# An encoder layer on one core: token operands of the FFN in overlapped rounds, and a four-tile last pass

## The chip, the core and the metric

The kernel runs on one core of a Trainium2 chip. Its engines are TensorE (PE, matrix products), VectorE (DVE), ScalarE (ACT), GpSimd (POOL) and SyncE (SP), which here issues every transfer. Each engine works through its own list of instructions in order and waits at semaphores for the others. The metric is the device time of one execution in microseconds.

## The reference, cut to what matters

One layer of a streaming encoder over 1024 tokens of width 1024, in float32, with a feed-forward width of 2816.

```python
x = x + 0.5 * _swiglu(_rmsnorm(x, n1_g[l]), ffn1_w_in[l], ffn1_w_out[l])
h = _rmsnorm(x, n2_g[l])
...   # one projection h @ w_in, then two attention branches o_a and o_b
merged = jax.nn.sigmoid(ga) * (o_a @ w_branch_a[l]) + jax.nn.sigmoid(gb) * (o_b @ w_branch_b[l])
x = x + merged @ w_out[l]
x = x + 0.5 * _swiglu(_rmsnorm(x, n3_g[l]), ffn2_w_in[l], ffn2_w_out[l])
return _rmsnorm(x, nf_g)
```

Here `_swiglu(x)` is `(silu(x @ gate) * (x @ up)) @ w_out`, and `_rmsnorm` divides each row by the root of its mean square and multiplies by a gain.

## The kernel before

Every product is made of three TensorE matmuls, since each operand is split into a high part (a cast on ScalarE, L82) and a remainder (a subtraction, L83, on VectorE, or on GpSimd where `w_eng` says so). The stages follow each other: FFN 1, a norm with its transposes (`norm_behind`), the projection with gates, attention A and B, the merge, FFN 2 and the final norm.

**First half of an FFN** (`ffn_in`). The product of tokens and input weights uses a form with seven block products in place of eight. Its token operands are b11, b21, b22 and four differences t1 to t4; they are made by `pair_operands` for four pairs of row tiles (p and p+4). For each pair: ScalarE squares both tiles (`rstds`, L166), VectorE normalises them (L244), GpSimd and VectorE make two differences each (L246 to L249, into two raw buffers), and TensorE transposes the seven operands in 28 steps of 128 columns (L254), each group of four into one bank named S, which ScalarE and VectorE then split. The weights have seven operands too, made by `ffn_weights` for each of NF = 22 column blocks i. Block i=0 is done in two halves of 256 columns, so that its first half needs pairs 0 and 1 alone: 14 products of 12 matmuls (L292). Later blocks take 512 columns. For i=0 GpSimd makes the remainders of the weights, later VectorE.

**Second half** (`out_rows`). A pass over two column tiles f adds to each of 8 row tiles, in two halves of 512 columns, a group of six matmuls (L118), and VectorE adds the bank into x (L226). The last pass of FFN 2 is taken row tile by row tile, each followed by its final norm (`scaled`) and the write of the output; GpSimd does two multiplications (L181, L182) for row tiles 1, 3 and 5, VectorE one instruction (L184) for the others. In the merge, column tiles go in pairs too, but the last two, i=6 and i=7, make a pass each (groups of three matmuls), the very last row tile by row tile, with `pair_operands` of FFN 2 after every pair.

**What sets the order.** The instruction order on each engine is laid out when the kernel is built, by a scheduler that runs the instructions through a timeline; code order and the pools' buffers bound it. All weights and some scratch come through one ring of five raw buffers of 128 x 1024 (`raw()`): a load into one waits until its last reader is done. The weight differences and the junk output of the Squares have a pool of their own, `sm`.

Of the kernel before, what the change touches and what calls it, by code (L numbers as in the profile page):

```python
# [43 lines left out]
class Layer:  # L44
# [114 lines left out]
    def rstds(self, tiles):  # L159
# [77 lines left out]
    def pair_operands(self, ops, x0, x1, gb, p):  # L237
# [12 lines left out]
        for n, src in (("b11", x0[:, :h]), ("b21", x0[:, h:]), ("b22", x1[:, h:]), ("t2", ta[:, h:]),  # L250
                       ("t1", ta[:, :h]), ("t3", tb[:, :h]), ("t4", tb[:, h:])):
            pt = self.bank("S")
# [6 lines left out]
    def ffn_weights(self, w_in, i):  # L259
# [5 lines left out]
        rg, ru = self.raw(), self.raw()  # L265
        for r, c in ((rg, i * P), (ru, F + i * P)):
            self.dma(r.rearrange("p (k c) -> p k c", k=KT), w_in[:, c:c + P].rearrange("(k p) c -> p k c", p=P))
        sm = [self.sm.tile([P, h], F32, tag=f"s{j}", name=self.uid(f"s{j}"), bufs=1) for j in range(4)]
        a11, a12, a21, a22 = rg[:, :h], rg[:, h:], ru[:, :h], ru[:, h:]
        for out, x, y, op in ((sm[0], a21, a22, ALU.add), (sm[1], sm[0], a11, ALU.subtract),  # L270
                              (sm[2], a11, a21, ALU.subtract), (sm[3], a12, sm[1], ALU.subtract)):
            nc.gpsimd.tensor_tensor(out, x, y, op)
        for j, src in enumerate((a11, a12, sm[1], sm[0], sm[2], sm[3], a22)):
            w = self.wp.tile([P, 2, h], F32R, tag=("whi", "wlo")[j % 2], name=self.uid("wop"), bufs=3)
            self.split(w[:, 0], w[:, 1], src, self.w_eng)
            yield w

    def ffn_in(self, w_in, ops, ph, g_d, first):
# [16 lines left out]
        for i in range(NF):  # L295
            self.w_eng = nc.gpsimd if i == 0 else nc.vector
            m = 256 if i == 0 else 512
            if i == 0:
                pairs = first()
                next(pairs)  # L300
                ws = list(self.ffn_weights(w_in, i))
                next(pairs, None)
            else:
                ws = self.ffn_weights(w_in, i)
            gh, gl = (ph.tile([P, SEQ], F32R, tag="t4", name=self.uid("g"), bufs=4) for _ in range(2))
# [34 lines left out]
    def ffn(self, x_d, w_in, w_out, g_d, ex, es_ex, first):  # L340
# [4 lines left out]
        kept = self.ffn_in(w_in, ops, ph, g_d, (lambda: iter((None,))) if first is None else lambda: first(ops, ph))  # L345
# [22 lines left out]
        for n, f in enumerate(range(0, NF - 2, 2)):  # L368
            cur = load((xo, go)[n % 2], f), weights(f)
            if f < NF - 4:  # L370
                self.out_rows(x, *cur, 0.5, range(NT))

# [461 lines left out]
    def merge(self, x, x1_d, gates_d, bra_d, ob, w_b, w_out, last, pool, pre):  # L834
# [3 lines left out]
        for i in range(KT):  # L838
            wh, wl = self.weights_cols(w_b, i * P, (i + 1) * P)
            gp, nb = (last, 1) if i == KT - 1 else (pool, 3)  # L840
# [26 lines left out]
            if len(cur) == 2 or i >= KT - 2:  # L867
                prev = (cur, [self.weights((w_out[f * P:(f + 1) * P, :], D)) for f in range(i + 1 - len(cur), i + 1)])
# [3 lines left out]
    def run(self):  # L872
# [14 lines left out]
        self.sm, es_sm = self.open("sm", bufs=1)  # L887
        ex, es_ex = self.open("ex", bufs=1, side="right")

        def first(ops, ph):  # L890
            xs = {}

            def load(ts):
                for t in ts:
                    xs[t] = ph.tile([P, D], F32, tag="t4", name=self.uid("x0"), bufs=4)
# [161 lines left out]
```

## Time and profile before

| | us |
|---|---|
| median of 3 runs | 2418.46 (2418.17 to 2420.24) |
| the profiled execution | 2418.89 |
| its span | 2417.1 |
| TensorE busy in the span | 2268.7 |
| VectorE busy | 1570.6 |
| ScalarE busy | 1015.6 |
| GpSimd busy | 572.2 |

Outside the span lie 1.8 us of the profiled execution. A timeline row gives the start, the duration, the engine, the line in the code, the operation with output and inputs, a count where equal neighbours are joined, and in brackets the idle time before it and who ended it. A row of windows gives the stretch, its length, busy time and number of instructions of PE, PEld (weight loads), DVE, ACT and POOL, then the granted TensorE clock as a share of full speed, the busy share of the DMA engines and GB/s; with a line as a filter, it has TensorE's share for that line alone. A row of a line gives count, shortest, median and longest duration in ns, and the first and last start. A row of instructions by line and shape gives the busy time and mean ns, and a row of transfers their number, KB of one, and median us from issue to landing.

### The profile page before, as it was taken

To read this page: it belongs to the slowest core of one execution; us is meant where nothing else is said; L and a number is where in the kernel's file an instruction comes from. 1 tells how busy PE (TensorE), PEld (TensorE's weight loads), DVE (VectorE), ACT (ScalarE), POOL (GpSimd) and SP (SyncE) were. 2 spreads that over 40 slices of the span, in tenths; PEclk is the share of its full clock that TensorE was granted. 3 is DMA by queue.
4 is the path that set the end of the run, shared out by engine and by line. 5 is a ranking of instruction groups with operands and counts; after the bars stand their busy time and mean duration, and the time that the engine had idled before them with its cause. 6 is when DMAs were issued, how large, how long until landed. Compare 5 with 4: busy or idle time off the path is not lost. (4 is left out here: it accounts for less than half of the span.)

```text
span 2417.1 us, 30580 instructions
## 1 busy us (share of the span) xinstructions
PE 2268.7 (94%) x10928; PEld 1894.5 (78%) x10928; DVE 1570.6 (65%) x2962; ACT 1015.6 (42%) x1973; POOL 572.2 (24%) x482
## 2 busy tenths in 40 slices
PE   3999999999999999998989999998699999999997
PEld 3877777778887987787778887876688888878886
DVE  5655555555656469798894388577665666656656
ACT  5444444420014554667734487532444444430002
POOL 3433333200014000222320143121433333310001
PEclk9999999999999999999999999998899999999999
DMA  3333333353422124455423241651333333354332
GB/s 104 116 105 105 105 105 105 105 212 145 157 93 104 36 75 120 106 131 133 119 67 98 100 157 40 217 171 48 105 104 114 105 105 105 117 197 166 127 117 105
DMA packets 204216, 280.81 MB, mean 116 GB/s; under 512 B 12064, under 2 KB 150304, under 8 KB 203552
## 3 DMA queue, kind: packets, MB, share of 16 engines
q1 hardware_dynamic: 204064, 278.86, 35.0%
q8 instruction: 86, 1.41, 0.2%
q14 instruction: 66, 0.54, 0.1%
HBM read 186.55 MB, written 79.69 MB: 110 GB/s over the span
## 5 line engine op out<-in xcount | busy, mean ns | idle before, releaser
L226 DVE SCALAR_TENSOR_TENSOR x<-S,x 128x512 f32<-128x512 f32 x432 | 292.1, 689 | 203.2 <-PE S L118 202.3
L82 ACT CAST whi<-raw 128x1024 fp32r<-128x1024 f32 (+1 forms) x92 | 87.6, 976 | 444.4 <-PE S L118 370.1
L118 PE MATMUL S<-wlo,goh 128*128 128x512 f32 x640 | 249.3, 389 | 0.0
L118 PE MATMUL S<-whi,gol 128*128 128x512 f32 x640 | 249.2, 389 | 0.0
L118 PE MATMUL S<-whi,goh 128*128 128x512 f32 x640 | 245.5, 394 | 3.4 <-DVE bigB L83 1.5
L292 PE MATMUL mm<-bigA,wop 128*128 128x512 f32 (+1 forms) x736 | 236.5, 384 | 10.8 <-ACT e L316 10.8
L83 DVE TENSOR_TENSOR wop<-s,wop 128x512 fp32r<-128x512 f32 x168 | 168.3, 1002 | 119.1 <-ACT wop L82 115.8
L292 PE MATMUL S<-bigA,wop 128*128 128x512 f32 (+1 forms) x736 | 233.0, 380 | 0.0
L83 DVE TENSOR_TENSOR wop<-raw,wop 128x512 fp32r<-128x512 f32 x126 | 114.1, 917 | 169.1 <-ACT wop L82 169.1
L83 POOL TENSOR_TENSOR wlo<-raw,whi 128x1024 fp32r<-128x1024 f32 (+1 forms) x32 | 68.2, 2130 | 524.8 <-ACT whi L82 516.1
L292 PEld LDWEIGHTS mm<-bigA,wop 128*128 128x128 f32 x736 | 136.6, 188 | 46.4 <-ACT e L316 20.3
L82 ACT CAST wop<-s 128x512 fp32r<-128x512 f32 x176 | 109.2, 622 | 142.4 <-PE mm L292 45.6
L118 PE MATMUL mm<-bigA,whi 128*128 128x512 f32 x384 | 155.3, 404 | 12.5 <-ACT whi L82 6.7
L292 PEld LDWEIGHTS S<-bigA,wop 128*128 128x128 f32 x736 | 136.5, 188 | 26.2
L118 PE MATMUL mm<-bigA,wlo 128*128 128x512 f32 x384 | 154.5, 403 | 2.3 <-POOL wlo L83 2.3
L323 POOL TENSOR_TENSOR e<-e,e 128x512 f32<-128x512 f32 (+1 forms) x46 | 57.2, 1243 | 419.1 <-ACT e L322 419.1
L118 PE MATMUL mm<-bigB,whi 128*128 128x512 f32 x384 | 154.7, 403 | 0.1
L118 PEld LDWEIGHTS S<-whi,goh 128*128 128x128 f32 x640 | 120.1, 188 | 35.9 <-DVE x L226 8.5
L586 POOL TENSOR_SCALAR p<-p,z 128x640 f32<-128x640 f32 (+7 forms) x128 | 92.7, 729 | 208.1 <-DVE z L585 141.4
L118 PEld LDWEIGHTS S<-whi,gol 128*128 128x128 f32 x640 | 120.2, 188 | 25.2
L292 PE MATMUL mm<-bigB,wop 128*128 128x512 f32 (+1 forms) x368 | 139.9, 380 | 0.0
L292 PE MATMUL S<-bigB,wop 128*128 128x512 f32 (+1 forms) x368 | 139.7, 380 | 0.0
(248 smaller groups left out, 5370.0 us busy)
## 6 DMA issues: line engine op xcount, KB each, us to landing
raw<-in_ffn_w_in_dram SPq DMA_DIRECT2D x88, 512.0 KB, 4.2
g_d<-g SPq DMA_DIRECT2D x80, 512.0 KB, 4.8
raw<-in_ffn_w_out_dram SPq DMA_DIRECT2D x44, 512.0 KB, 6.9
goh<-g_d SPq DMA_DIRECT2D x40, 512.0 KB, 5.1
gol<-g_d SPq DMA_DIRECT2D x40, 512.0 KB, 6.1
raw<-in_w_in_dram SPq DMA_DIRECT2D x28, 512.0 KB, 5.9
x<-in_x_dram SPq DMA_DIRECT2D x16, 512.0 KB, 6.6
x_d<-x SPq DMA_DIRECT2D x16, 512.0 KB, 2.6
```

Source lines behind the costliest of these rows:

```text
L82: self.nc.scalar.copy(hi, src)
L83: (eng or self.nc.vector).tensor_tensor(lo, src, hi.bitcast(F32), ALU.subtract)
L118: nc.tensor.matmul(out, lhsT=a, rhs=b, start=(i == 0), stop=(i == len(steps) - 1))
L226: nc.vector.scalar_tensor_tensor(xs, po, scale, xs, ALU.mult, ALU.add)
L292: nc.tensor.matmul(out, lhsT=l, rhs=r, start=start and j == 0, stop=j == len(steps) - 1, skip_group_check=True)
L323: nc.gpsimd.tensor_tensor(e3, e3, e5, ALU.add)
L586: nc.gpsimd.tensor_scalar(p, p, z, 1.0, ALU.mult, ALU.mult)
```

## The change

Five things are changed.

1. **Token operands.** `pair_operands` becomes a generator in two parts: norm and scaling, then differences and transposes. A new `all_operands` runs the first part of pair p+1 ahead of the second part of pair p. All four differences are GpSimd's, t1 and t4 in place, so a pair needs one raw buffer; the transposes go to the banks named mm and tp in turn instead of S.
2. **Weights.** `ffn_weights` takes raw buffers that are already being loaded, and makes its differences in place and in one tile `s` (two buffers for i>0, a raw buffer for i=0). For i=0 it is called after pair 2's second step in FFN 1, and ahead of `ffn` in FFN 2, whose first load is issued ahead of the merge's last rows.
3. **Junk.** The Squares write into a raw buffer, and the pool `sm` is gone. FFN 1 has six x tiles in flight instead of four.
4. **Merge.** The last two column tiles make one pass with groups of six matmuls.
5. **FFN 2's end.** The last pass takes four tiles f (16 to 19). g and weights of f = 18 and 19 wait in a spare 4 MB tile. Every final scaling is VectorE's.

```diff
@@ rstds
-            junk = self.sm.tile([P, D], BF16, tag="s0", name=self.uid("junk"), bufs=1)
+            junk = self.raw()
@@ pair_operands
-        ta, tb = self.raw(), self.raw()
-        nc.gpsimd.tensor_tensor(ta[:, :h], x1[:, :h], x0[:, :h], ALU.subtract)
-        nc.vector.tensor_tensor(ta[:, h:], x1[:, h:], ta[:, :h], ALU.subtract)
-        nc.gpsimd.tensor_tensor(tb[:, :h], x1[:, h:], x1[:, :h], ALU.subtract)
-        nc.vector.tensor_tensor(tb[:, h:], x0[:, h:], ta[:, h:], ALU.subtract)
...
-            pt = self.bank("S")
+        yield
+        b11, b21, b12, b22 = x0[:, :h], x0[:, h:], x1[:, :h], x1[:, h:]
+        tt = self.raw()
+        t3, t2 = tt[:, :h], tt[:, h:]
...
+        def sub(out, x, y):
+            nc.gpsimd.tensor_tensor(out, x, y, ALU.subtract)
+            return out
...
+            pt = self.bank(("mm", "tp")[turns % 2])
...
+        sub(t3, b22, b12)
+        turn("b11", b11)
+        turn("b21", b21)
+        turn("b22", b22)
+        t1 = sub(b12, b12, b11)
+        turn("t3", t3)
+        sub(t2, b22, t1)
+        turn("t1", t1)
+        turn("t2", t2)
+        turn("t4", sub(b21, b21, t2))
+
+    def all_operands(self, ops, tiles, gb, rows=None):
+
+        todo = []
+        for p in range(4):
+            if rows is not None:
+                rows(p)
+            g = self.pair_operands(ops, *tiles(p), gb, p)
+            next(g)
+            todo.append(g)
+            if p > 0:
+                next(todo[p - 1], None)
+            yield
+        next(todo[3], None)
@@ ffn
-        for n, f in enumerate(range(0, NF - 2, 2)):
+        end = 4 if big else 2
+        for n, f in enumerate(range(0, NF - 4, 2)):
             cur = load((xo, go)[n % 2], f), weights(f)
-            if f < NF - 4:
+            if f < NF - 2 - end:
                 self.out_rows(x, *cur, 0.5, range(NT))
+        f = NF - 4
+        if big:
+            spare = self.hp.tile([P, 8, SEQ], F32R, tag="bigA", name=self.uid("spare"))
...
+            cur = cur[0] + g, cur[1] + w
@@ the merge
-            if len(cur) == 2 or i >= KT - 2:
+            if len(cur) == 2:
@@ first (FFN 1)
+            raws = self.ffn_raw(io["ffn1_w_in"], 0)
+            load(pairs[4:6])
+            made = self.all_operands(ops, lambda p: (xs[p], xs[p + 4]), gb)
+            for p in range(4):
+                if p == 3:
+                    load(pairs[6:])
+                next(made)
+                if p == 2:
+                    self.w_eng = nc.gpsimd
+                    ws = list(self.ffn_weights(raws, self.raw()))
+            next(made, None)
@@ the final norm
-            self.scaled(x[:, t, :], x[:, t, :], gf, fin, t in (1, 3, 5))
+            self.scaled(x[:, t, :], x[:, t, :], gf, fin, False)
```

What this does to the order of instructions is seen at three places. Rows name line, operation, output and inputs; before, L246 and L248 are the token subtractions and L272 those of the weights, after, L252 and L309; L83 is a remainder.

GpSimd at the start, after the constants. Before:

```order
L83 TENSOR_TENSOR wop_130<-raw_118,wop_130 128x512
L83 TENSOR_TENSOR wop_133<-raw_118,wop_133 128x512
L272 TENSOR_TENSOR s_13_122<-raw_119 128x512
L272 TENSOR_TENSOR s_15_124<-raw_118,raw_119 128x512
L272 TENSOR_TENSOR s_14_123<-s_13_122,raw_118 128x512
L83 TENSOR_TENSOR wop_139<-s_13_122,wop_139 128x512
L272 TENSOR_TENSOR s_16_125<-raw_118,s_14_123 128x512
L83 TENSOR_TENSOR wop_136<-s_14_123,wop_136 128x512
L83 TENSOR_TENSOR wop_142<-s_15_124,wop_142 128x512
L83 TENSOR_TENSOR wop_145<-s_16_125,wop_145 128x512
L246 TENSOR_TENSOR raw_169<-x_7_110,x_6_108 128x512
L248 TENSOR_TENSOR raw_170<-x_7_110 128x512
```

After:

```order
L252 TENSOR_TENSOR raw_155<-x_7_107 128x512
L252 TENSOR_TENSOR x_7_107<-x_7_107,x_6_105 128x512
L83 TENSOR_TENSOR wop_283<-raw_115,wop_283 128x512
L83 TENSOR_TENSOR wop_286<-raw_115,wop_286 128x512
L252 TENSOR_TENSOR raw_155<-x_7_107 128x512
L252 TENSOR_TENSOR raw_225<-x_10_113 128x512
L252 TENSOR_TENSOR x_6_105<-x_6_105,raw_155 128x512
L252 TENSOR_TENSOR x_10_113<-x_10_113,x_9_111 128x512
L309 TENSOR_TENSOR raw_279<-raw_116 128x512
L252 TENSOR_TENSOR raw_225<-x_10_113 128x512
L309 TENSOR_TENSOR raw_279<-raw_279,raw_115 128x512
L309 TENSOR_TENSOR raw_116<-raw_115,raw_116 128x512
```

The token subtractions stood behind all weight work of block 0 and came two a pair; they now come first, four a pair, mixed with the weight work, and pair 0 and pair 1 stand close together.

TensorE at the end of the merge (L118 are the matmuls of the rows, S a bank, whi and wlo weights, gh and gl the gated activations; L254 and L260 transposes). Before, from the last matmuls of pair 0's rows on:

```order
L118 MATMUL S_15328<-whi_15295,gh_15160 128x512
L118 MATMUL S_15328<-wlo_15296,gh_15160 128x512
L118 MATMUL S_15328<-whi_15295,gl_15161 128x512
L254 MATMUL S_15356<-ident,x_14296 128x128 x4
L254 MATMUL S_15363<-ident,x_14296 128x128 x4
L254 MATMUL S_15370<-ident,x_14296 128x128 x4
L254 MATMUL S_15377<-ident,raw_15350 128x128 x4
L254 MATMUL S_15384<-ident,raw_15350 128x128 x4
L254 MATMUL S_15391<-ident,raw_15351 128x128 x4
L254 MATMUL S_15398<-ident,raw_15351 128x128 x4
L118 MATMUL S_15405<-whi_15295,gh_15160 128x512
```

After, where the first transposes stand:

```order
L118 MATMUL S_15321<-whi_15138,gh_15077 128x512
L118 MATMUL S_15321<-wlo_15139,gh_15077 128x512
L118 MATMUL S_15321<-whi_15138,gl_15078 128x512
L260 MATMUL tp_15261<-ident,x_14219 128x128 x4
L260 MATMUL mm_15268<-ident,x_14219 128x128 x4
L260 MATMUL tp_15275<-ident,x_14219 128x128 x4
L118 MATMUL S_15330<-whi_15132,gh_14889 128x512
L118 MATMUL S_15330<-wlo_15133,gh_14889 128x512
L118 MATMUL S_15330<-whi_15132,gl_14890 128x512
L118 MATMUL S_15330<-whi_15138,gh_15077 128x512
L118 MATMUL S_15330<-wlo_15139,gh_15077 128x512
L118 MATMUL S_15330<-whi_15138,gl_15078 128x512
```

Before, all seven transpose groups of a pair stood together between its rows and those of the next pair. Now the first three groups of pair 0 stand in the middle of pair 2's rows, and rows of six matmuls go on between them and the rest.

SP at the end of FFN 1 (x_d are the writes of x1, raw from in_w_in the first gate weights, goh and gol the g tiles of the last pass). Before:

```order
L79 DMA goh_5005<-g_d_91 128x1024
L79 DMA gol_5006<-g_d_91 128x1024
L79 DMA raw_5560<-in_w_in_dram 128x8x128
L79 DMA goh_5149<-g_d_91 128x1024
L79 DMA gol_5150<-g_d_91 128x1024
L79 DMA goh_5153<-g_d_91 128x1024
L79 DMA gol_5154<-g_d_91 128x1024
L79 DMA x_d<-x_3664 128x1024 x8
L79 DMA raw_5626<-in_w_in_dram 128x584
```

After:

```order
L79 DMA goh_4932<-g_d_91 128x1024
L79 DMA gol_4933<-g_d_91 128x1024
L79 DMA goh_5076<-g_d_91 128x1024
L79 DMA gol_5077<-g_d_91 128x1024
L79 DMA goh_5080<-g_d_91 128x1024
L79 DMA gol_5081<-g_d_91 128x1024
L79 DMA x_d<-x_3591 128x1024 x8
L79 DMA raw_5486<-in_w_in_dram 128x8x128
L79 DMA raw_5552<-in_w_in_dram 128x584
```

The load of the first gate weights stood ahead of the last four g loads and the eight writes; it now stands behind them.

## Rows read from the trace of the kernel before

**Rows 1.** Page, table of engines
```profile
PE 2268.7 (94%) x10928; PEld 1894.5 (78%) x10928; DVE 1570.6 (65%) x2962; ACT 1015.6 (42%) x1973; POOL 572.2 (24%) x482
```

**Rows 2.** Windows, all engines: the start, the merge, the tail
```profile
0.00:60.00 60.00, 22.48 (x136) 19.32 (x136) 33.07 (x65) 30.75 (x55) 20.87 (x22) 1.00 0.34 102
1672.50:1690.00 17.50, 10.09 (x39) 8.72 (x40) 12.75 (x22) 7.46 (x14) 2.50 (x2) 0.61 0.15 61
2390.00:2400.00 10.00, 8.47 (x36) 6.06 (x34) 9.61 (x29) 3.92 (x9) 3.85 (x3) 1.00 0.26 105
```

**Rows 3.** Timeline of TensorE over the first 62 us
```profile
28.48 2.79 PE L254 MATMUL S<-ident,x 128*128 128x128 f32 x12 [28.48 <-DVE x L244]
...
47.80 1.68 PE L292 MATMUL mm<-t,wop 128*128 128x256 f32 x12
...
60.55 0.42 PE L292 MATMUL mm<-b,wop 128*128 128x256 f32 x1 [0.68 <-ACT b L82]
```

**Rows 4.** First 40 us: transfer of x (transfers); timeline of ScalarE, then VectorE
```profile
x<-in_x_dram SPq DMA_DIRECT2D x6, 512.0 KB, 4.2
...
20.31 1.06 ACT L166 ACTIVATE junk<-x 128x1024 bf16<-128x1024 f32 x1
...
27.05 2.48 DVE L244 SCALAR_TENSOR_TENSOR x<-x,rs,raw 128x1024 f32<-128x1024 f32 x2
```

**Rows 5.** Timeline of TensorE at the merge; its matmuls there by line and shape
```profile
1678.32 2.82 PE L254 MATMUL S<-ident,x 128*128 128x128 f32 x12 [5.85 <-DVE x L244]
1682.73 3.74 PE L254 MATMUL S<-ident,raw 128*128 128x128 f32 x16 [1.59 <-DVE raw L247]
...
1695.20 2.35 PE L254 MATMUL S<-ident,x 128*128 128x128 f32 x12 [4.78 <-DVE x L244]
...
L118 PE MATMUL S<-wlo,gh 128*128 128x512 f32 x12 | 5.2, 436 | 0.0
```

**Rows 6.** Timeline of the tail: TensorE, GpSimd, VectorE
```profile
2403.93 0.39 PE L118 MATMUL S<-whi,gol 128*128 128x512 f32 x1
...
2402.09 2.40 POOL L181 TENSOR_TENSOR x<-x,gain 128x1024 f32<-128x1024 f32 x1
...
2402.36 2.15 DVE L173 TENSOR_TENSOR rs<-rs,rt 128x1 f32<-128x1 f32 x1
...
2407.01 0.68 DVE L226 SCALAR_TENSOR_TENSOR x<-S,x 128x512 f32<-128x512 f32 x1
...
2412.13 1.28 DVE L184 SCALAR_TENSOR_TENSOR x<-x,rs,gain 128x1024 f32<-128x1024 f32 x1
```

**Rows 7.** Windows of line 292 on TensorE alone
```profile
0.00:60.00 60.00, 7.78 (x48) 1.00 0.34 102
1733.00:1741.00 8.00, 7.30 (x49) 0.79 0.36 106
```

**Rows 8.** Timeline near 29.6 us: GpSimd, VectorE
```profile
29.61 1.27 POOL L246 TENSOR_TENSOR raw<-x,x 128x512 f32<-128x512 f32 x1 [4.44 <-DVE rs L169]
...
29.64 1.25 DVE L170 TENSOR_TENSOR rt<-rs 128x2 f32<-128x2 f32 x1
```

**Rows 9.** Lines 244, 247, 170; line 83 of VectorE from 28 to 62 us
```profile
L244 DVE SCALAR_TENSOR_TENSOR x<-x,rs,raw x16: 1276/1280/1285, 27.1 to 1727.0; 128x1024 f32<-128x1024 f32 x16
...
L247 DVE TENSOR_TENSOR raw<-x,raw x8: 676/1620/1736, 32.9 to 1729.8; 128x512 f32<-128x512 f32 x8
...
L170 DVE TENSOR_TENSOR rt<-rs x24: 142/160/2252, 25.9 to 2411.4; 128x1 f32<-128x1 f32 x16, 128x2 f32<-128x2 f32 x8
...
L83 DVE TENSOR_TENSOR bigB<-S,bigA x12: 674/682/692, 37.1 to 60.8; 128x512 fp32r<-128x512 f32 x12
```

**Rows 10.** Transition to the projection: SP, TensorE; the page's transfers
```profile
721.61 26.01 SPq L79 DMA_DIRECT2D x_d<-x  x8
...
747.80 0.47 PE L118 MATMUL mm<-bigA,whi 128*128 128x512 f32 x1
...
raw<-in_w_in_dram SPq DMA_DIRECT2D x28, 512.0 KB, 5.9
```

More of the change, by code (lines that the diff above doesn't have):

```diff
@@ L268, in ffn_weights, with sub @@
[L268 removed]
+        rg, ru = raws
         a11, a12, a21, a22 = rg[:, :h], rg[:, h:], ru[:, :h], ru[:, h:]
[L270 to L271 removed]
+        s1, s2 = s[:, :h], s[:, h:]
+        def sub(out, x, y, op=ALU.subtract):
             nc.gpsimd.tensor_tensor(out, x, y, op)
[L273 removed]
+        sub(s1, a21, a22, ALU.add)
@@ L295, in ffn_in @@
         for i in range(NF):
-            self.w_eng = nc.gpsimd if i == 0 else nc.vector
             m = 256 if i == 0 else 512
[L298 to L305, printed above, removed]
+            if i > 0:
+                self.w_eng = nc.vector
+                ws = self.ffn_weights(self.ffn_raw(w_in, i),
+                                      ph.tile([P, 1024], F32, tag="s", name=self.uid("s"), bufs=2))
+            elif ws is None:
+                ws = first(ops, ph)
+            gh, gl = (ph.tile([P, SEQ], F32R, tag="t4", name=self.uid("g"), bufs=self.t4) for _ in range(2))
             for c in range(0, 512, m):
@@ L367, in ffn @@
         go, es_go = self.open("go", bufs=1)
-        for n, f in enumerate(range(0, NF - 2, 2)):
+        end = 4 if big else 2
+        for n, f in enumerate(range(0, NF - 4, 2)):
             cur = load((xo, go)[n % 2], f), weights(f)
-            if f < NF - 4:
+            if f < NF - 2 - end:
                 self.out_rows(x, *cur, 0.5, range(NT))
+        f = NF - 4
+        if big:
+            spare = self.hp.tile([P, 8, SEQ], F32R, tag="bigA", name=self.uid("spare"))
+            g, w = [(spare[:, 2 * j], spare[:, 2 * j + 1]) for j in range(2)], []
+            for j in range(2):
+                for h in range(2):
+                    self.dma(g[j][h], g_d[f + j, h])
+                raw = self.raw()
+                self.dma(raw, w_out[(f + j) * P:(f + j + 1) * P, :])
+                w.append((spare[:, 4 + 2 * j], spare[:, 5 + 2 * j]))
+                self.split(*w[j], raw)
+            cur = cur[0] + g, cur[1] + w
+        else:
+            cur = load(go, f), weights(f)
         def close():
@@ L866, in merge @@
                 prev = None
-            if len(cur) == 2 or i >= KT - 2:
-                prev = (cur, [self.weights((w_out[f * P:(f + 1) * P, :], D)) for f in range(i + 1 - len(cur), i + 1)])
+            if len(cur) == 2:
+                prev = (cur, [self.weights((w_out[f * P:(f + 1) * P, :], D)) for f in (i - 1, i)])
                 cur = []
@@ L992, in run, with pair_rows @@
         self.dma(gb, io["n3_g"].partition_broadcast(P))
-        for t in pairs:
-            rows((t,))
-            self.dma(x2_d[t], x[:, t, :])
-            if t >= 4:
-                self.pair_operands(ops2, x[:, t - 4, :], x[:, t, :], gb, t - 4)
+        raws = self.ffn_raw(io["ffn2_w_in"], 0)
+        def pair_rows(p):
+            for t in (p, p + 4):
+                rows((t,))
+                self.dma(x2_d[t], x[:, t, :])
+        made = self.all_operands(ops2, lambda p: (x[:, p, :], x[:, p + 4, :]), gb, pair_rows)
+        for _ in range(4):
+            next(made)
+        self.w_eng = nc.gpsimd
+        ws = list(self.ffn_weights(raws, self.raw()))
+        next(made, None)
         es_m1.close()
-        x, rows, close = self.ffn(x2_d, io["ffn2_w_in"], io["ffn2_w_out"], g_d[1], ops2, es_ex, None)
+        x, rows, close = self.ffn(x2_d, io["ffn2_w_in"], io["ffn2_w_out"], g_d[1], ops2, es_ex, None, ws, True)
         fin, es_fin = self.open("fin", bufs=1)
@@ L1007, in run @@
         close()
-        es_sm.close()
 @with_exitstack
```

41 lines of the change are left out of this document (22 added, 19 removed).

## The prediction

> **What bounds the kernel now.** I read the page's table of engines first: TensorE is busy 94% of the span, VectorE 65%, GpSimd 24% [rows 1]. So the kernel is bound by TensorE, and an edit pays only where TensorE waits. The windows show where that is. In the first 60 us TensorE works 22.48 us, so 37.5 us are idle; between 1672.5 and 1690 it works 10.09 of 17.5, at a granted clock of 0.61; between 2390 and 2400 it works 8.47 of 10 [rows 2]. These are the three places the diff touches. Elsewhere the order of TensorE's instructions in the two feed-forward stages is the same in both kernels, so those hundreds of microseconds cancel.
>
> The timeline says who is waited for. At the start the first transposes begin at 28.48, released by VectorE's normalisation of the pair (L244), and TensorE runs without a gap from 60.55 [rows 3]. The cause lies earlier: the x tiles land in 4.2 us, but ScalarE squares the first one only at 20.31, behind casts of first-stage weights, and the normalisation comes at 27.05 [rows 4]. At the second FFN every pair of row tiles shows the same pattern: TensorE waits for the normalisation (5.85 us, then 4.78) and for a subtraction (1.59) [rows 5]; there are four such pairs, the eight waits add up to 27.3 us, and the pairs follow each other every 16 us or so, one after the other. At the end TensorE's last matmul starts at 2403.93 and ends by 2404.4, but the last evacuation runs at 2407.01, the last scaling at 2412.13, and the span closes 3.7 us after it, at 2417.1 [rows 6].
>
> **Start of FFN 1.** End of column block i=0 before: by 60 us TensorE had done 48 of the 168 matmuls of block 0 in 7.78 us [rows 7], and 88 of the 112 transposes (136 instructions in 22.48 us in all [rows 2], so 14.7 us for these). Left are 120 matmuls at 0.12 us (twelve take about 1.5 us [rows 3]) = 14.4, and 24 transposes at 0.17 = 4.0; from 60.55 that is 79.
>
> After: the Squares move ahead of the weights, so pair 0 is normalised at about 12.3: x issued at 0.7, landed about 5, then the 7 us from Square (20.31) to the end of its first scaling (27.05 plus 1.25), a little less since a cast and another Square stood in between [rows 4], and 1.2 for the second tile. What then sets the pace is GpSimd: it now does all 16 token subtractions, 4 weight subtractions and 7 remainders of the first block. Up to the subtraction that the first b11 product stands behind on TensorE (t2 of pair 3) those are 25 instructions at 1.25 us (its subtraction L246 takes 1.27 [rows 8]) = 31.3. VectorE's six scalings of pairs 1 to 3, 1.2 us each = 7.2, come in between (below). 12.3 + 31.3 + 7.2 = 50.8, with transposes about 52. Behind it stand 13 products of 12 matmuls (18.7 us; one is done earlier) and three groups of transposes, about 1.4: 72. Gain 7 (79 to 72). Bounds: 14, if the scalings cost GpSimd nothing; 0, if each of the 25 waits 0.3 us for small VectorE work as well.
>
> The 7.2 rests on this: in the trace two-input VectorE instructions do not run beside a GpSimd one. The tiny L170, normally 0.16 us, took 1.25 at 29.64 while GpSimd's L246 ran from 29.61; the evacuations, one input of which lies in PSUM, stayed at 674 to 692 ns [rows 9]. The scaling L244 itself never ran beside a busy GpSimd: 1276 to 1285 ns in all 16 cases [rows 8, 9]. So its behaviour there is inferred from L170 and L247 (676 to 1736 ns [rows 9]), the nearest rows. The Trainium skill (SBUF — State Buffer, section "SBUF: two separate sides") states that the two engines share one port pair as an exclusive lock, held for a whole instruction, and that a VectorE operation with two SBUF inputs takes part; by that rule L244 blocks and is blocked, which is the 52, and without it the chain ends near 45. The rows on L170 agree with it; no row shows L244.
>
> The four weight subtractions and remainders also feed i=1, whose raw buffers are freed late. By replay of the order its loads land about 51 and its products start after 72: hidden by 15 us and more.
>
> **Norm to projection.** The ring of five raw buffers now also takes the junk of the Squares, and the load of the first gate weights has moved behind the eight writes of x1 on the SP queue. Those writes are issued from 721.61 on for 26.01 us; before, 24 gate matmuls filled TensorE from 747.80 to 754.1, between transposes (their first [rows 10]). Now the load leaves at about 747.7, lands 5.9 later [rows 10], then cast and remainder, about 1 and 2.4: 757. TensorE has these 24 matmuls ahead of the last transposes and waits on them. At most their whole cover (24 x 0.23 = 5.5) and a bit is lost, +6; at least nothing, if the transposes of the last tiles were late anyway. I take +3.5, nearer to the whole because they stand in front in TensorE's order.
>
> **Merge and start of FFN 2.** The last two column tiles become one pass with six matmuls per group: eight row tiles of 2 x 6 x 0.227 = 2.72 us, starting about 1658.8 (of the two old passes' 96 matmuls 36, three lines of 12 [rows 5], come after TensorE's first wait, which begins at 1678.32 - 5.85 = 1672.47; the 60 before it take 13.6). 16 evacuations on VectorE vanish, hidden beside TensorE before too: nothing. Pair 0's rows are complete at 1664, its scaling at about 1671, while TensorE still has rows of later pairs to do: the first wait of 5.85 goes. Each further pair costs two row tiles (5.4) and seven groups of transposes (16 take 3.7 us [rows 5], so 6.5): the scalings end at about 1671, 1682.5 and 1695. After that of pair 2 GpSimd still has 16 instructions, 8 of tokens and 8 of weights: 20 us, and two scalings of pair 3 between, 2.4: 1717.4. Behind it stand again 20.1 us of products and transposes: block 0 ends at 1737.5. Before: by 1741 some 50 of 168 products were done (49 counted from 1733 to 1741 [rows 7]), so 118 x 0.12 = 14.2 more: 1755. Gain 17.8. Bounds: 28, if pair 2 is scaled 7 us earlier and the lock costs nothing; 8, if the pairs keep coming 16 us apart as now. The clock follows: it was granted at 0.61 of full speed in the first of these stretches [rows 2], where TensorE paused; that is part of both ends. The loads for i=1 wait for raw buffers freed at about 1717 and land 1722.5; their first use is about 1735: 12 us of cover.
>
> **Tail.** The last pass now spans four tiles of f, 5.44 us of TensorE per row tile against some 3.6 of VectorE (two evacuations, one scaling, six small ones). TensorE's three waits there, 1.5 us (10 less 8.47 [rows 2]), go. All scalings are VectorE's, so GpSimd's 2.40 us multiplication no longer holds up the small product at 2402.36 (2.15 us) [rows 6]. After the last matmul remain: evacuation 0.7, Square 1.25, mean, root and five small steps 1.7, scaling 1.28, write 3.7 = 8.6, against 12.7 now. Gain 4.1 + 1.5 = 5.7, between 4 and 7. The extra 4 MB for f = 18 and 19 is read hundreds of microseconds ahead, and its casts fall on ScalarE, 42% busy [rows 1]: nothing. Small reorderings inside the attention stage: nothing, up to 3 either way.
>
> **Sum.** -7 + 3.5 - 17.8 - 5.7 = -27. From the profiled execution's 2418.9 that is 2391.9; the median of the runs lies 0.4 lower, so 2391.5.
>
> **Rivals.**
> 1. *The lock eats it.* GpSimd waits about 0.4 us at each instruction (the nearest row is VectorE's L247, 0.68 alone and up to 1.74 beside L248 [rows 9]), and the pairs in effect still come one after another. FFN 1 gains nothing, FFN 2 only 17.8 - 6.4 = 11.4 or less: 0 + 3.5 - 11 - 5.7 = -13, 2405. For it: GpSimd's chain is long and VectorE's small steps have two inputs. Against: the evacuations, most of VectorE's work there, were not held up. It also covers the case that the change doesn't do what it says, the rounds not overlapping: FFN 2 then keeps its 16 us pitch and gains 8.
> 2. *No lock for the scaling.* -14 + 3.5 - 25 - 5.7 = -41: 2377.5. The 1285 ns maximum speaks for it, but only because the case never arose.
> 3. *Slower.* One mechanism: all subtractions and remainders now stand in a single file on GpSimd, with transposes and products behind, where before products of the first half filled gaps. If an instruction there costs 2.5 us instead of 1.25 (each alternating with a VectorE one), FFN 1's first product comes at 12.3 + 62.5 + 1 = 76, block 0 ends at 96: +16.5; FFN 2's at 1695 + 40 = 1735, block 0 at 1755: 0. With +3.5 and -5.7: +14, 2433. It decides from about 1.9 us per instruction on, since 41 instructions x 0.65 eat the 27. The longest two-input row here is about 1.75, so it is unlikely.
>
> **Chances.** Forecast (2380 to 2400) 0.55; rival 1 (2400 to 2411) 0.23; rival 2 (below 2380) 0.10; slower 0.07; within 0.2% of the old time, between rivals 1 and 3, 0.05. Differences below 0.2%, about 5 us, can't be told from none here. Faster 0.88, same 0.05, slower 0.07. The range reaches to rival 2's and rival 1's values: 2377 to 2408.
>
> **What would show it.** First transposes near 11 to 13 instead of 28.48, GpSimd near solid from 12 to 55, first run of b11 products near 52: the start. A TensorE gap of 3 to 6 us near 750: the gates. Near 1672 no 5.85 us wait, no gap-free TensorE later than 1718: the merge. Last scaling within 5 us of the last matmul: the tail. L244 above 1.3 us or GpSimd waiting for it: the lock. Wrong if GpSimd's pitch there is not near 1.25, or if the loads behind the raw ring are waited for.

## The result, and the profile after

The changed kernel takes 2391.03 us (median of 4 runs, 2389.85 to 2392.12) against 2419.35 for the kernel before on the same chip: a ratio of 0.9884, with a 95% interval from 0.9869 to 0.9898. 2391.5 was forecast, faster, with a range of 2377 to 2408. The profiled execution's span is 2388.2 us; before it was 2417.1, so 28.9 us went.

Where they went is read best at marks that both traces have. SP's transfers do for that, since each waits for the end of a stage. Here are six marks (SP's timeline; start, duration), first of the kernel before, then of the kernel after: the first write of g of FFN 1's block 1, the first write of x1 (before: [rows 10]), the second write of gates (a row of a line that covers the writes from the second on; its first start counts), the load of x into the merge, and FFN 2's writes of g of blocks 1 and 3.

```profile
108.65 0.34 SPq L79 DMA_DIRECT2D g_d<-g  x1
...
L79 SPq DMA_DIRECT2D gates_d<-raw x15: 320/339/1390, 838.4 to 1393.8; - x15
...
1548.39 5.09 SPq L79 DMA_DIRECT2D x<-x_d  x6
...
1787.57 0.34 SPq L79 DMA_DIRECT2D g_d<-g  x1
...
1825.65 0.34 SPq L79 DMA_DIRECT2D g_d<-g  x1
```

```profile
104.45 0.34 SPq L79 DMA_DIRECT2D g_d<-g  x1
...
717.47 26.02 SPq L79 DMA_DIRECT2D x_d<-x  x8
...
L79 SPq DMA_DIRECT2D gates_d<-raw x15: 320/339/1625, 837.3 to 1391.8; - x15
...
1548.78 4.55 SPq L79 DMA_DIRECT2D x<-x_d  x6
...
1765.34 0.34 SPq L79 DMA_DIRECT2D g_d<-g  x1
...
1803.42 0.34 SPq L79 DMA_DIRECT2D g_d<-g  x1
```

| mark | before, us | after, us | difference | gained or lost since the mark above |
|---|---|---|---|---|
| FFN 1, write of g, block 1 | 108.65 | 104.45 | -4.2 | -4.2 |
| first write of x1 | 721.61 | 717.47 | -4.1 | 0 |
| projection, second write of gates | 838.4 | 837.3 | -1.1 | +3.0 |
| load of x into the merge | 1548.39 | 1548.78 | +0.4 | +1.5 |
| FFN 2, write of g, block 1 | 1787.57 | 1765.34 | -22.2 | -22.6 |
| FFN 2, write of g, block 3 | 1825.65 | 1803.42 | -22.2 | 0 |
| end of the span | 2417.1 | 2388.2 | -28.9 | -6.7 |

Forecast were -7 at the start, +3.5 at the projection, nothing in the attention, -17.8 at the merge and -5.7 at the end. Each of the four changes has the right sign. That the sum is nearer than its terms is luck: a start that gained 3 us less and an attention that lost 1.5 stand against a merge that gained 5 more.

**Start.** TensorE's first transposes come at 10.91 (28.48 before [rows 3]), as foreseen. The first run of b11 products is at 55.95, where 52 was forecast. TensorE's timeline, then GpSimd's, VectorE's and one row of ScalarE's:

```profile
10.91 1.09 PE L260 MATMUL tp<-ident,x 128*128 128x128 f32 x4 [10.91 <-DVE x L244]
...
34.12 1.97 PE L260 MATMUL tp<-ident,x 128*128 128x128 f32 x8 [4.54 <-DVE bigB L83]
...
55.95 1.70 PE L335 MATMUL mm<-b,wop 128*128 128x256 f32 x12
...
12.11 1.27 POOL L252 TENSOR_TENSOR raw<-x 128x512 f32<-128x512 f32 x1 [10.81 <-DVE x L244]
...
21.57 1.27 POOL L252 TENSOR_TENSOR raw<-x 128x512 f32<-128x512 f32 x1 [3.15 <-DVE x L244]
...
30.14 2.24 POOL L83 TENSOR_TENSOR wop<-raw,wop 128x512 fp32r<-128x512 f32 x1
32.35 2.25 POOL L252 TENSOR_TENSOR x<-x,raw 128x512 f32<-128x512 f32 x1
...
49.18 1.27 POOL L252 TENSOR_TENSOR raw<-x 128x512 f32<-128x512 f32 x1 [2.93 <-DVE x L244]
...
52.98 1.28 POOL L252 TENSOR_TENSOR raw<-x 128x512 f32<-128x512 f32 x1
...
16.01 1.21 DVE L172 TENSOR_SCALAR rt<-rt 128x2 f32<-128x2 f32 x1
...
29.01 4.45 DVE L244 SCALAR_TENSOR_TENSOR x<-x,rs,raw 128x1024 f32<-128x1024 f32 x2
...
43.65 1.26 DVE L170 TENSOR_TENSOR rt<-rs 128x2 f32<-128x2 f32 x1
...
35.27 0.59 ACT L82 CAST bigA<-tp 128x512 fp32r<-128x512 f32 x1 [5.07 <-PE tp L260]
```

GpSimd starts at 12.11 (12.3 was forecast) and ends the subtraction t2 of pair 3 at 54.26: 42.1 us for 25 instructions. 31 of these are its own work, 11 are waits, where I had allowed 7.2. The row at 29.01 holds what no row of before could show [rows 9]: two scalings in 4.45 us instead of 2.48, while GpSimd's 30.14 and 32.35 take 2.24 and 2.25 instead of 1.27. Each waits for the other, in turns. The longer part is waiting outright, 3.15 and 2.93 us for scalings of pairs 1 and 3 that were late. For pair 1 the reason is that VectorE had first waited for GpSimd at its small steps (1.21 us at 16.01). For pair 3 such waits make some 2 us (1.26 at 43.65, where 0.16 is usual, and 1.12 at the next L172), and its Squares were late besides: they stand on ScalarE behind a cast that waited 5.07 us for TensorE (35.27). TensorE waits behind the two slow scalings as well (4.54 us at 34.12, for an evacuation on VectorE).

**Merge.** The first long wait is gone; of eight waits, 27.3 us in all [rows 5], nine smaller ones of 13.5 us remain. The windows show the stretch with its cost (columns as in [rows 2]); the rows under them are TensorE's, GpSimd's and VectorE's.

```profile
1672.50:1690.00 17.50, 13.44 (x79) 10.78 (x77) 17.27 (x37) 11.76 (x25) 8.60 (x7) 0.99 0.34 138
1690.00:1706.00 16.00, 9.73 (x40) 8.18 (x40) 11.64 (x14) 5.87 (x11) 14.21 (x10) 0.50 0.01 2
...
1690.59 1.09 PE L260 MATMUL tp<-ident,x 128*128 128x128 f32 x4 [2.68 <-DVE x L244]
...
1701.19 0.80 PE L335 MATMUL S<-bigA,wop 128*128 128x256 f32 x2 [4.11 <-POOL wop L83]
...
1713.01 1.96 PE L335 MATMUL mm<-b,wop 128*128 128x256 f32 x12
...
1691.79 1.27 POOL L252 TENSOR_TENSOR raw<-x 128x512 f32<-128x512 f32 x1 [6.00 <-DVE rt L170]
...
1695.47 4.45 POOL L309 TENSOR_TENSOR raw<-raw,raw 128x512 f32<-128x512 f32 x2
...
1710.92 1.27 POOL L252 TENSOR_TENSOR raw<-x 128x512 f32<-128x512 f32 x1
...
1668.10 2.48 DVE L244 SCALAR_TENSOR_TENSOR x<-x,rs,raw 128x1024 f32<-128x1024 f32 x2
...
1689.17 2.47 DVE L244 SCALAR_TENSOR_TENSOR x<-x,rs,raw 128x1024 f32<-128x1024 f32 x2
...
1694.82 3.97 DVE L244 SCALAR_TENSOR_TENSOR x<-x,rs,raw 128x1024 f32<-128x1024 f32 x2
```

The scalings of pairs 0, 2 and 3 end at 1670.6, 1691.6 and 1698.8. Then GpSimd works from 1691.79 to 1712.2 with no gap between its instructions (two of them take 4.45 us instead of 2.5, beside the scalings of pair 3), and the first b11 products follow at 1713.0 (1717.4 was forecast). TensorE works 13.44 of the first 17.5 us instead of 10.09 [rows 2]. From 1690 to 1706, where it works 9.73 of 16 us and waits 4.11 of them for GpSimd, the granted clock is 0.50, the lower of its two levels.

**Projection.** The wait named in the prediction is there: 4.35 us for the cast of the first gate weights, which itself waited for the load (TensorE, then ScalarE).

```profile
749.25 0.80 PE L118 MATMUL mm<-bigA,whi 128*128 128x512 f32 x1 [4.35 <-ACT whi L82]
...
748.15 1.04 ACT L82 CAST whi<-raw 128x1024 fp32r<-128x1024 f32 x1 [1.67 <-DMA raw<-in_w_in_dram]
```

**Tail.** TensorE's last six matmuls start at 2377.85 and end at 2379.4, the last evacuation follows at 2379.88 and the last scaling at 2383.23; the span ends at 2388.2. That is 8.8 us after the last matmul, against 12.7 before [rows 6]. (TensorE, then VectorE; six matmuls are one row.)

```profile
2377.85 1.52 PE L118 MATMUL S<-spare 128*128 128x512 f32 x6
...
2379.88 0.68 DVE L226 SCALAR_TENSOR_TENSOR x<-S,x 128x512 f32<-128x512 f32 x1
...
2383.23 1.28 DVE L184 SCALAR_TENSOR_TENSOR x<-x,rs,gain 128x1024 f32<-128x1024 f32 x1
```

### The profile page after: what moved, and what is told of

It reads as the page before. It is cut to its first block, busy times and chain, and to the rows that moved or that the text cites. A ratio compares the mean times of both kernels' runs of the same rounds, so it can differ in the third digit from the quotient of the medians.

```text
span 2388.2 us, 30574 instructions
## 1 busy us (share of the span) xinstructions
PE 2265.6 (95%) x10928; PEld 1893.1 (79%) x10928; DVE 1517.9 (64%) x2917; ACT 1010.3 (42%) x1971; POOL 589.8 (25%) x492
## 5 line engine op out<-in xcount | busy, mean ns | idle before, releaser
L226 DVE SCALAR_TENSOR_TENSOR x<-S,x 128x512 f32<-128x512 f32 x400 | 270.6, 689 | 201.6 <-PE S L118 200.8
L83 DVE TENSOR_TENSOR wop<-raw,wop 128x512 fp32r<-128x512 f32 x210 | 150.3, 723 | 204.5 <-ACT wop L82 203.9
L118 PE MATMUL S<-wlo,goh 128*128 128x512 f32 x608 | 236.8, 389 | 0.0
L118 PE MATMUL S<-whi,gol 128*128 128x512 f32 x608 | 236.7, 389 | 0.0
L118 PE MATMUL S<-whi,goh 128*128 128x512 f32 x608 | 232.9, 393 | 1.9 <-DVE bigB L83 1.5
L82 ACT CAST wop<-raw 128x512 fp32r<-128x512 f32 x224 | 137.4, 625 | 103.7 <-PE mm L335 44.9
L118 PE MATMUL mm<-bigA,whi 128*128 128x512 f32 x384 | 156.0, 406 | 16.0 <-ACT whi L82 10.0
L83 DVE TENSOR_TENSOR wop<-s,wop 128x512 fp32r<-128x512 f32 x84 | 91.5, 1090 | 115.7 <-ACT wop L82 115.4
L118 PE MATMUL mm<-bigA,wlo 128*128 128x512 f32 x384 | 155.2, 405 | 2.1 <-POOL wlo L83 2.1
L118 PE MATMUL mm<-bigB,whi 128*128 128x512 f32 x384 | 154.9, 403 | 0.2 <-DVE bigB L83 0.2
L83 POOL TENSOR_TENSOR wlo<-raw,whi 128x1024 fp32r<-128x1024 f32 (+1 forms) x32 | 67.7, 2114 | 301.1 <-ACT whi L82 292.3
L118 PEld LDWEIGHTS S<-whi,goh 128*128 128x128 f32 x608 | 114.1, 188 | 31.5 <-DVE x L226 6.3
L309 POOL TENSOR_TENSOR raw<-raw,s 128x512 f32<-128x512 f32 x42 | 54.6, 1300 | 332.4 <-DVE wop L83 332.4
L335 PE MATMUL mm<-b,wop 128*128 128x512 f32 (+1 forms) x552 | 134.5, 381 | 0.0
```

What stands on the lines that cost most here:

```text
L82: self.nc.scalar.copy(hi, src)
L83: (eng or self.nc.vector).tensor_tensor(lo, src, hi.bitcast(F32), ALU.subtract)
L118: nc.tensor.matmul(out, lhsT=a, rhs=b, start=(i == 0), stop=(i == len(steps) - 1))
L226: nc.vector.scalar_tensor_tensor(xs, po, scale, xs, ALU.mult, ALU.add)
L335: nc.tensor.matmul(out, lhsT=l, rhs=r, start=start and j == 0, stop=j == len(steps) - 1, skip_group_check=True)
```

## Experiments on parts of the change

Theory A was that of the prediction: what sets the end of the first block is GpSimd's single file, stretched by the waits in turn with VectorE, and at the merge the joint pass and the overlap of the rounds. Its rival B put the limit on VectorE, or held that the moved work was hidden anyway.

**Subtractions back on VectorE.**

```diff
-        sub(t2, b22, t1)
+        nc.vector.tensor_tensor(t2, b22, t1, ALU.subtract)
...
-        turn("t4", sub(b21, b21, t2))
+        nc.vector.tensor_tensor(b21, b21, t2, ALU.subtract)
+        turn("t4", b21)
```

> The changed kernel with the differences t2 and t4 of every pair back on VectorE; t1 and t3 stay on GpSimd. Theory A (GpSimd's single file, stretched by the shared port, sets the end of the first weight block in FFN 1; there the chain is 25 instructions of 1.25 us plus 11 us of waits): seven fewer before the first run of b11 products, 9 us, of which VectorE's own two-input waits give some back; block 0 ends 3 to 6 us earlier in FFN 1 and 2 to 4 in FFN 2, 2383 to 2387. Theory B (the file on GpSimd is not what sets the end, but the scalings and evacuations on VectorE, which are loaded further here): within 2 us in both places or later, 2389 to 2396.

**Remainders of block 0's weights on VectorE.**

```diff
-                    self.w_eng = nc.gpsimd
+                    self.w_eng = nc.vector
                     ws = list(self.ffn_weights(raws, self.raw()))
...
-        self.w_eng = nc.gpsimd
+        self.w_eng = nc.vector
         ws = list(self.ffn_weights(raws, self.raw()))
```

> The changed kernel with the remainders of block 0's weights on VectorE in both FFNs; all subtractions stay on GpSimd. Theory A: six instructions leave GpSimd's file ahead of the first b11 products in FFN 1, 7.5 us, but VectorE's remainders have two inputs in the scratch memory and alternate with GpSimd; block 0 ends 3 to 5 us earlier in FFN 1, and 3 to 6 in FFN 2 where ten weight instructions stood behind the last scalings: 2381 to 2386. Theory B: no change within 2 us, or later by up to 5, 2389 to 2396.

By their medians both were slower than the changed kernel: 2396.1 us (ratio to before 0.9899, interval 0.9884 to 0.9914) and 2398.94 (0.9914, 0.9894 to 0.9935), though these intervals overlap with its own. By the totals theory B would have won, with both just beyond its upper bound of 2396. The marks say otherwise. The first run of b11 products comes at 51.68 and 51.98 instead of 55.95, and the mark in FFN 1's block 1 at 100.18 and 100.34 instead of 104.45: 4.3 and 4.1 us earlier, inside A's bounds. From the merge's load of x to FFN 2's block 1 it is 214.7 and 213.5 us instead of 216.6, which points the same way, but isn't clean, because the rounds of FFN 2 behind the mark have another order; the kernels with the order rule, below, repeat it. The loss lies behind that mark, where neither edit touches anything: two rounds of FFN 2 took 39.6 us (1754.71 to 1794.32 in the first) instead of 38.08, which is 13.8 us over the 18 rounds from block 1 to block 19. In the first kernel the attention ran 3.9 us shorter, too, without an edit there. SP's writes of g in the first of the two, and TensorE's matmuls of one group, FFN 2 from 1850 to 2140 us (busy, mean ns, and behind the second bar the idle time before them), in the changed kernel and then in the first of the two:

```profile
1754.71 0.34 SPq L79 DMA_DIRECT2D g_d<-g  x1
...
1794.32 0.34 SPq L79 DMA_DIRECT2D g_d<-g  x1
```

```profile
L335 PE MATMUL mm<-bigA,wop 128*128 128x512 f32 x250 | 82.4, 390 | 1.4 <-ACT e L357 1.4
```

```profile
L336 PE MATMUL mm<-bigA,wop 128*128 128x512 f32 x237 | 79.9, 398 | 7.0 <-ACT e L358 7.0
```

So an unforeseen thing had to be settled before the parts could be compared: what makes a round 19.04 or 19.80 us.

**The order within a round.** In the kernel before and in the changed one FFN 1 runs at 19.80 us a round and FFN 2 at 19.04, with the same 84 matmuls (twelve follow each other in 2.72 us, 0.2267 each, and 84 x 0.2267 = 19.04: no idle time at all). In FFN 1's order one matmul of t1 stands between the last of t2 and the first of t3, which goes into the same bank, and ScalarE's copy has to empty that bank in between (TensorE, then ScalarE, changed kernel):

```profile
206.70 2.88 PE L335 MATMUL mm<-t,wop 128*128 128x512 f32 x12
209.42 0.39 PE L335 MATMUL S<-bigA,wop 128*128 128x512 f32 x1
210.26 0.50 PE L335 MATMUL mm<-bigA,wop 128*128 128x512 f32 x1 [0.45 <-ACT e L357]
...
209.62 0.58 ACT L357 COPY e<-mm 128x512 f32<-128x512 f32 x1 [4.54 <-PE mm L335]
```

An order rule, for block 1 on, puts the whole product b21 behind t2:

```diff
...   # product() returns its last matmul
-                product(by, next(w), ops["b21"], cols, True)
-                product(bx, next(w), ops["t2"], cols, False)
+                wy = next(w)
+                last = product(bx, next(w), ops["t2"], cols, False)
                 nc.scalar.copy(e2, bx)
+                with self.behind(0, last if i > 0 else None):
+                    product(by, wy, ops["b21"], cols, True)
```

> The changed kernel with one ordering rule more: from block 1 on, the product with b21 may stand on TensorE only behind the product with t2. In FFN 1's rounds (19.80 us each) b21 stands ahead of t1 and 11 of t1's 12 matmuls stand ahead of t2, so that one matmul is left between t2 and t3, and t3's first waits for ScalarE's copy of the bank; in FFN 2's (19.04) b21 stands between t2 and t3. Theory P (that order alone is the difference): FFN 1's rounds go to 19.04, 21 x 0.76 = 16 us, about 2375. Rival Q (ScalarE's load or FFN 1's six x tiles set the pitch, the wait moves elsewhere): within 3 us, 2388 to 2394.

2374.44 us, 0.9815 (0.9797 to 0.9834): theory P, 16.6 us faster than the changed kernel by the medians. FFN 1's rounds now take 19.04 us, and by the first write of x1 15.3 us are gained (702.14 against 717.47). t2 (mm), b21 (tp) and t3 (mm) now follow each other without a wait:

```profile
196.12 2.88 PE L335 MATMUL mm<-t,wop 128*128 128x512 f32 x12
198.84 2.88 PE L335 MATMUL tp<-b,wop 128*128 128x512 f32 x12
201.56 0.39 PE L335 MATMUL mm<-bigA,wop 128*128 128x512 f32 x1
...
702.14 26.01 SPq L79 DMA_DIRECT2D x_d<-x  x8
```

The rule alone on the kernel before:

> The kernel before with nothing but the order rule. Its FFN 1 also runs at 19.80 us a round with the same wait of 0.45 for ScalarE's copy, its FFN 2 at 19.04. If the rule's gain is its own and not the change's: FFN 1 gains 21 x 0.76 = 16 us, ratio 0.993 to 0.994, and the difference of change and before stays near 28 with the rule in both. If it hangs on the changed weights' path: less than 5 us.

2403.09 us, 0.9928 (0.9911 to 0.9945). The gain, 16.1 us by the medians, is the rule's own; here, too, 15.3 us of it lie ahead of the first write of x1. With the rule in both kernels the change is worth 28.7 us (2403.09 less 2374.44), as without it (28.3). So the 28 are the change's own.

What is left of the rule's gain behind x1, 1.4 to 1.6 us of span, is a balance of larger shifts, and they limit what marks can tell. In FFN 2, whose pitch stays at 19.04, the rule brings the mark of block 1 forward by 4.3 us, counted from the load of x (6.9 in the kernel before), and the stretch from block 19's mark to the end is 5.0 us longer (4.9). That looks like a write of g that has moved within the round. So marks at blocks are compared here only between kernels with the same order within a round.

**The last two tiles of the merge in a pass each.**

```diff
-            gp, nb = (last, 2) if i >= KT - 2 else (pool, 3)
+            gp, nb = (last, 1) if i == KT - 1 else (pool, 3)
...
-            if len(cur) == 2:
+            if len(cur) == 2 or i >= KT - 2:
...   # and a pass takes the tiles that are there
```

> The changed kernel with the last two column tiles of the merge in a pass each, as before. Theory A (the joint pass completes pair 0's rows 8 us earlier and gives twice the TensorE work behind which the scalings of the pairs run): the scalings start 4 to 6 us later, and FFN 2's block 0 ends 4 to 8 us later: 2395 to 2399. Theory B (the joint pass only takes 16 evacuations off VectorE, which were hidden): within 2 us, 2389 to 2393.

2419.32 us, 0.999 (0.9981 to 0.9999): within about 0.1% of the kernel before. Neither theory had that. At FFN 2's block 1 the mark lay 9.5 us later than in the changed kernel, and the rest came after it: this kernel, too, had slow rounds in FFN 2. With the order rule that falls away:

> The same rule, and the last two column tiles of the merge in a pass each. Without the rule that cost 25.7 us of span. Theory P (15 of them are 20 rounds of FFN 2 in the slow order, which the scheduler fell into, and about 10 the merge itself): about 10 above the kernel with the rule alone, 2384 to 2387 if that is at 2375. Rival Q (all of it is the merge, by clock and waits): 25 above, 2398 to 2402.

2384.67 us, 0.9855 (0.9838 to 0.9871): 10.2 us above the kernel with the rule alone, as theory P had it. From the load of x to FFN 2's block 1 it is 11.7 us longer (224.0 against 212.3). So the joint pass brings 10 to 12 of the 22.6 us at the merge. The scalings show how. Both kernels load x into the merge at 1531 us, but pair 0 is normalised at 1653.26 with the joint pass and at 1669.98 without it, much later than the 4 to 6 us expected, since its rows are complete only in the very last pass. TensorE then has no rows of later pairs to do and waits at the transposes, 6.09 us at one of them, for an evacuation on VectorE behind two scalings that took 4.45 us. VectorE's scalings with the joint pass, then without it, with TensorE's row:

```profile
1653.26 2.48 DVE L244 SCALAR_TENSOR_TENSOR x<-x,rs,raw 128x1024 f32<-128x1024 f32 x2
```

```profile
1669.98 2.47 DVE L244 SCALAR_TENSOR_TENSOR x<-x,rs,raw 128x1024 f32<-128x1024 f32 x2
...
1695.06 4.45 DVE L244 SCALAR_TENSOR_TENSOR x<-x,rs,raw 128x1024 f32<-128x1024 f32 x2
...
1700.16 1.12 PE L260 MATMUL tp<-ident,x 128*128 128x128 f32 x4 [6.09 <-DVE bigB L83]
```

**Rounds not overlapped in code.**

```diff
-            if p > 0:
-                next(todo[p - 1], None)
+            next(g, None)
             yield
-        next(todo[3], None)
```

> The changed kernel with each pair's second part straight behind its first, so that the rounds don't overlap in code; everything else as changed. Theory A (the overlap of rounds is what takes TensorE's waits away): the waits of 4 to 5 us per pair come back at the merge, FFN 2's block 0 ends 8 to 12 us later, FFN 1's 0 to 4: 2399 to 2407. Theory B (the scheduler reorders the instructions anyway, and the gain comes from the joint pass, the early weights and the banks): within 4 us, 2387 to 2395.

2393.56 us, 0.9887 (0.9872 to 0.9902), 3.6 us more of span: theory B. FFN 2's rounds were fast here, so the totals can be compared. The overlap that gives the change its name is worth 1 us at the start (105.42 against 104.45) and about 1.4 at the merge (217.9 us from the load of x to block 1, against 216.6). The scheduler moves instructions across the pairs by itself: in this kernel VectorE starts the scalings of pair 1 at 20.47, ahead of the last evacuations of pair 0 (22.87). That it is the new banks and buffers which let it was not tested.

**Junk in place.** The norm before the projection squares into its own output tile, not into a raw buffer:

```diff
-            junk = self.raw()
-            nc.scalar.activation(junk, xt, AF.Square, accum_out=ms[:, i:i + 1])
+            out = self.raw() if junk is None else junk
+            nc.scalar.activation(out, xt, AF.Square, accum_out=ms[:, i:i + 1])
...
-        r, = self.rstds([xt])
+        r, = self.rstds([xt], out if on_pool else None)
```

> The changed kernel with the Squares of the norm before the projection writing into that norm's own output tile instead of a raw buffer; the load of the first gate weights then stands ahead of the last four g loads and the x1 writes again. Theory: the wait of 4.35 and 3 us at about 749 goes, and 3 us come back: 2387 to 2389; GpSimd's gain multiplication then waits for the Square, which may cost 1. Rival (the projection's start is bound by the last tiles' normalisation in any case): within 1 us, 2390 to 2392.

2411.29 us, 0.996 (0.9946 to 0.9975). The profiled execution, 2404.32, is the shortest of five; its span is 14.3 us above that of the changed kernel. 13.7 us are slow rounds in FFN 2 (39.6 us for two), which say nothing of the edit. The 7 us from this execution to the median were not traced. At the projection nothing was won either: from the first write of x1 to the second write of gates 120.7 us, against 119.8 in the changed kernel and 116.8 before. The load went ahead again, so the raw ring had moved it, as the prediction said. But GpSimd's multiplication by the gain now waits for the Square, and TensorE waits for GpSimd. (GpSimd, then TensorE.)

```profile
751.71 4.66 POOL L181 TENSOR_TENSOR xn<-x,gain 128x1024 f32<-128x1024 f32 x2 [2.88 <-ACT xn L166]
...
758.31 3.67 PE L195 MATMUL S<-ident,xn 128*128 128x128 f32 x16 [6.78 <-POOL xn L182]
```

One wait took the place of the other. What the late load costs by itself therefore stays open; it is known only that the stretch as a whole lost 3.0 us.

**The tail alone**, on the kernel before:

```diff
-            self.scaled(x[:, t, :], x[:, t, :], gf, fin, t in (1, 3, 5))
+            self.scaled(x[:, t, :], x[:, t, :], gf, fin, False)
...   # and the last pass over four tiles, as in the change
```

> The kernel before with nothing but FFN 2's end: the last pass over four tiles with the spare tile, and all final scalings on VectorE. The prediction gave it 4.1 (after the last matmul) and 1.5 (TensorE's waits), 5.7 in all, between 4 and 7; the trace of the changed kernel shows 6.7. Theory: 5.7 to 6.7 faster than before, ratio 0.9972 to 0.9976. Rival (the tail's gain depends on the rest of the change, or the early 4 MB load or its casts cost something): less than 3 us.

2414.61 us, 0.9977 (0.9967 to 0.9986), 5.3 us under the kernel before in the same series. From FFN 2's block 3 to the end of the span are 584.8 us, in the changed kernel 584.8 too, and 591.5 before. The 6.7 us hold wherever the tail is built in. The profiled execution, the longest of the ten (2410.90 to 2416.98), had lost 4.8 us by then, in stages that the edit doesn't touch, spread over the start, the projection, the attention and the merge.

**Both together: a faster kernel.** With the order rule the edits on GpSimd's file can be tried again; these kernels join the diffs shown above.

> The order rule together with block 0's weight remainders on VectorE. Alone the latter gained 4 us in each FFN's block 0, and lost 15 by FFN 2's rounds in the slow order, which the rule now forbids. If the two add up: 4 to 8 below the kernel with the rule alone, 2366 to 2371. If the start is already as early as the evacuations let it, no more than 2 below: 2372 to 2375.

> The order rule together with t2 and t4 back on VectorE. Alone the latter gained 4.3 us in FFN 1's block 0 and about 2 to 3 in FFN 2's. If these add up: 3 to 7 below the kernel with the rule alone, 2367 to 2372; else 2372 to 2375.

> The order rule, the remainders and t2 and t4 on VectorE; GpSimd keeps t1, t3 and the weight subtractions. If GpSimd's file is the limit: 6 to 10 below the rule alone, 2364 to 2369. If VectorE then becomes the limit of block 0 (23 more two-input instructions of 0.7 us, and each alternates with GpSimd): no better than the better of the two, 2367 to 2372.

| kernel | median, us | ratio to before (95%) | first b11 products at, us |
|---|---|---|---|
| changed kernel and rule | 2374.44 | 0.9815 (0.9797 to 0.9834) | 57.13 |
| and remainders on VectorE | 2365.39 | 0.9774 (0.9756 to 0.9793) | 51.92 |
| and t2, t4 on VectorE | 2368.19 | 0.9787 (0.9769 to 0.9805) | 51.63 |
| and both | 2367.93 | 0.9787 (0.9765 to 0.9809) | 53.00 |

Each takes 4 to 5.5 us at the start, and 3 between the load of x and FFN 2's block 1 (212.3 us with the rule alone; 209.2, 209.0 and 209.4). The lowest median is 53.8 us under the kernel before and some 26 under the changed one; the three can't be told apart, their intervals overlap. Both together gain no more than one. That fits a VectorE which is then the longer file, as the third expectation put it; the times alone don't show it. The first of the three came out 0.6 us beyond its bounds, on the better side.

## Why the prediction was right, point by point

- **What bounds the kernel.** TensorE, and only where it waits: held. The three places and the transition account for all but the 1.5 us that the attention lost. That the rounds cancel held for the two kernels; that they are safe did not, since four of the experiments fell into the slow order.
- **Start, -7.** The sign and mechanism were right, the size was not: -4.2. The mis-sized term is the 7.2 us of alternation with the scalings, which measured 11 in all: about 2 for the scalings of pair 2, 6.1 for those of pairs 1 and 3, which came late, and 2.8 for ScalarE's casts. I had counted what the lock costs GpSimd, not what it costs VectorE first and gives back to GpSimd as a late scaling. The two ends of block 0 were off, too: the last matmul with 256 columns starts at 87.46 before and 83.30 after, not at 79 and 72, since in both kernels three products of block 1 (36 matmuls with 512 columns, some 8.2 us) stand among those of block 0. The sum had left them out on both sides, and so they cancel. That GpSimd's file sets the end was shown: with six or seven instructions fewer in it the products came 4.0 to 5.5 us earlier.
- **The lock.** Inferred from L170 and L247, now seen: two scalings in 4.45 us. The Trainium skill (SBUF — State Buffer, "SBUF: two separate sides") has the same rule, an exclusive lock held for a whole instruction; the trace agrees.
- **Projection, +3.5.** Measured +3.0, with the wait where it was named. That it is the load's place in SP's queue alone isn't shown, since the one edit that moved the load back made another wait.
- **Merge, -17.8.** Measured -22.6. The pitch of the scalings was mis-sized: those of pairs 1 and 2 end 9.7 and 11.4 us behind the pair before, instead of 11.5 and 12.5, so that pair 2's ended at 1691.6 instead of 1695, and the first products came 4.4 us early. Of the cause I had said too little: the joint pass is 10 to 12 of it, the overlap about 1. What the remaining 10 or so come from (the weights made early, the banks, the buffers) was not taken apart. The subtractions and remainders on GpSimd are not among it: put back on VectorE, either saves 3 us there. The evacuations that vanish were rightly put at nothing.
- **Tail, -5.7.** Measured -6.7, and 6.7 again with the tail alone; 3.9 behind the last matmul and 1.5 of TensorE's waits make 5.4, and 1.3 I can't place.
- **The rivals.** The first (the lock eats it) was what the start did by half; the second (no lock) is refuted by the 4.45 us. The third needed 1.9 us per GpSimd instruction; at the start it was 42.1 / 25 = 1.7, not far off.

## What to carry to other kernels

A kernel whose order comes from a scheduler answers a local edit far away: compare marks of the stages, not totals, with marks that stand at the same place in the order of both kernels, and look for a steady loop that has changed its pitch, before an edit is judged. When work is moved to an engine whose instructions wait in turn with another's, count the wait in both directions, and the instruction that comes late because of it. A wait of half a microsecond in a loop of 21 rounds was worth more here (some 16 us) than the change's start and tail together (11).

## What the runs showed of the hardware

- VectorE instructions with a single tensor input can wait for GpSimd too: L172, a scale and offset of 128 x 2 numbers, took 1.21 us at 16.01, beside a GpSimd remainder, 0.72 and 1.12 at pairs 2 and 3, and 0.17 at 9.08, where GpSimd had nothing to do. Before, its longest was 170 ns; but L167, the same operation, took 1.30 there at 22.67, beside GpSimd remainders. The evacuations, with one input in PSUM, stayed at 675 to 693 ns. The Trainium skill (SBUF — State Buffer, "SBUF: two separate sides") counts VectorE's two-port performance modes among what the lock holds up, too; no row here shows whether L172 runs in one.
- The transposes that started early and with pauses ran at a lower granted clock: 0.74 over the first 60 us, where it was 1.00 before [rows 2], with TensorE busy 28.92 us instead of 22.48. Four transposes took 1.06 us at 11.79 and 0.60 at 54.99. In the kernel with the lowest median, where TensorE is busy 35.01 of these 60 us, it was 0.89. (Window of the changed kernel.)

```profile
0.00:60.00 60.00, 28.92 (x154) 23.81 (x155) 43.20 (x66) 30.75 (x58) 38.76 (x36) 0.74 0.45 134
```
